# Scatters over four gate tables in turns, and attention scores of two heads at a time

## The chip, the cores and the metric

The kernel runs on one core of one Trainium2 chip. The metric is device time in microseconds (us) of one execution; of the kernel before it is the median of three runs. One execution was also recorded by the hardware profiler, and every duration below is from that recording.

The core's engines work side by side, each through its own instructions in order: TensorE (PE; its weight loads are PEld), VectorE (DVE), ScalarE (ACT), GpSimd (POOL) and SyncE (SP). They wait for each other through semaphores. A DMA is issued by an engine, runs on the DMA engines, and lands later. PE writes into PSUM, from where ACT and DVE fetch results.

## The reference

Two transformer blocks over 256 tokens of width 2048, all in float32. The first block: attention with 16 "forgetting" heads and 16 dilated heads, an output projection, and then PEER, a layer that picks 128 of 16384 experts per token. The second block: sliding-window attention (12 heads), gated linear attention, stick-breaking attention (8 heads), an output projection and a squared-ReLU MLP.

```python
def peer(x, w_query, sub_keys, expert_down, expert_up):     # T = 256 tokens, 8 heads, top 16 of each
    q = (xt @ w_query).reshape(T, PEER_HEADS, 2, PEER_HALF)
    scores = jnp.einsum('thpc,hpnc->thpn', q, sub_keys)
    vals, idx = lax.top_k(scores, PEER_TOPK)
    cand = vals[..., 0, :, None] + vals[..., 1, None, :]    # 16 x 16 sums per head
    top_vals, top_c = lax.top_k(cand, PEER_TOPK)
    experts = i1 * PEER_N_KEYS + i2                         # 8 x 16 experts per token
    gates = jax.nn.softmax(top_vals)
    hdn = jax.nn.gelu(einsum('ted,td->te', expert_down[experts], x))
    return einsum('te,ted->td', gates * hdn, expert_up[experts])

def stick_breaking(q, k, v):                                # per head
    z = q @ k.T * scale
    between = reversed_cumsum(log_sigmoid(-z)) - log_sigmoid(-z)
    return where(strict, exp(log_sigmoid(z) + between), 0) @ v
```

## The kernel before

**The matrix products.** All large products run as one stream of steps on PE (class Gemm, function run). A step is half of a weight tile of 1 MB: SP loads the tile (raw), ACT rounds it to a high part (whi), DVE computes the low part (wlo <- raw, whi), and PE does 12 matmuls with 512 columns, or in the products called turned 8 with 512 and 8 with 256, into acc. Up to four steps are split ahead. The stages in order: projections of block one (96 steps), its output projection (32), the PEER query (32), the products with all of expert_down (256 steps in 16 chunks, called s1 below) and with all of expert_up (256 steps, s2), the projections of block two (80), its output projection (32) and the MLP (256).

**The rest rides along.** Everything else is written as generators in lanes (evac, main, tail, attn, choose, top, rows). After every PE step one round goes through the lanes; a generator emits some instructions and says with `yield n` how many rounds later it wants to go on. This settles at build time the order in which each engine gets its instructions. A virtual clock per engine (vt), advanced by a fixed price per instruction, decides a few things, such as whether a low part is given to POOL. Nearly all instructions carry line 195, that of the helper which records them; those that issue DMAs on POOL carry their own lines.

**PEER.** The kernel computes the products with all 16384 experts and multiplies by a table of gates that is zero for the experts not picked. For each of four query groups g and two token halves tt, a generator `choose` finds the 16 best of each head on DVE. Its 32 columns of experts and gates are then scattered by 32 indirect DMAs on POOL (line 1096), each of which adds one gate per token into a DRAM table. There are four tables, gates00, gates01, gates10 and gates11, chosen by g mod 2 and tt. Two scatters into one table must not overlap, so the second waits on POOL until the first has landed; scatters into different tables don't wait for each other. Before, each of the eight sets of 32 was a generator of its own in the lane rows (up to four active), which emitted one scatter per round. There are 256 scatters.

When s1 is nearly done, `weigh` fetches for each chunk c the activations (line 1124) and the rows of the four tables (line 1127) on POOL's queue, adds two halves on POOL (nb <- nb,nb), multiplies on DVE (nb <- nb,nb), and splits the result into xt, which s2 reads. The call for chunk 0 stands behind all scatters in POOL's order; its multiplication, and behind one more low part that of chunk 1, stand in DVE's order some 20 steps before the end of the 256 steps of s1, among the low parts of the weights.

**Attention.** Dilated, sliding-window and stick-breaking heads are worked in pairs: the 128 partitions of a tile qk hold two heads of 64 rows each. `dil_pair`, `swa_pair` and `stick_pair` transpose (aux <- const,nb), copy to qk, and then did one head per round: two score matmuls (aux <- qk, 64 rows deep, 128 and 256 columns), then the softmax on DVE and ACT, and a `tail` that transposes the probabilities and multiplies by v. In stick_head the scores z go through three ACT operations, two of DVE and a mask on POOL (nb <- nb,const) to l1m; two rounds later PE multiplies l1m by a triangle (aux <- nb,const, here called the suffix sums).

Of the kernel before, what the change touches and what calls it, by code (L numbers as in the profile page):

```python
# [10 lines left out]
I32 = mybir.dt.int32  # L11
U32 = mybir.dt.uint32
AF = mybir.ActivationFunctionType
OP = mybir.AluOpType
# [4 lines left out]
T = 256  # L19
# [5 lines left out]
CAND = [(0, 1, 16), (1, 1, 8), (2, 1, 5), (3, 1, 4), (4, 1, 3), (5, 3, 2), (8, 8, 1)]  # L25
NCAND = 50
CLAMP = 2.0
MATCH, PACE = 0.09, 2.0
SWA_ORDER = [0, 3, 1, 4, 2, 5, 6, 9, 7, 10, 8, 11]


# [177 lines left out]
class Build:  # L209
# [276 lines left out]
    def attend(self, p, v, out):  # L486

        nc = self.nc
        pt = self.aux([128, 384])
        for i in range(3):  # L490
            nc.tensor.transpose(pt[:, i * 128:(i + 1) * 128], p[:, i * 128:(i + 1) * 128], self.c("ident"))
        ps = p[:, :384]
        nc.vector.tensor_copy(ps, pt)
        yield 1
        po = self.aux([128, 2, 64])
        nc.tensor.matmul(po[:, 0, :], ps[:, :128], v(0), start=True, stop=True)
        nc.tensor.matmul(po[:, 1, :], ps[:, 128:256], v(0), start=True, stop=False)
        nc.tensor.matmul(po[:, 1, :], ps[:, 256:384], v(1), start=False, stop=True)
        nc.vector.tensor_tensor(out, po, p[:, 388:390, None].to_broadcast([128, 2, 64]), op=OP.mult)
        self.pss.give(p)  # L500

    def scores(self, qk, rows):
        nc = self.nc
        sc = self.aux([128, 384])
        nc.tensor.matmul(sc[:, :128], qk[rows, 0, :], qk[rows, 2, :], start=True, stop=True)
        nc.tensor.matmul(sc[:, 128:], qk[rows, 1, :], qk[rows, 2:4, :].rearrange("p a b -> p (a b)"),
                         start=True, stop=True)
        return sc

    def fox_head(self, h, st, cnt):  # L510
        nc = self.nc
        q, k, v = st["fq"], st["fk"], st["fv"]
        while "gate" not in st:
            yield 1
        qk = yield from self.get(self.qks, [128, 4, 128])
        pt = self.aux([128, 4, 128])
        for i, src in enumerate((q, k)):
            for tt in range(2):
                nc.tensor.transpose(pt[:66, 2 * i + tt, :], src[:, tt, h, :], self.c("ident"))
        nc.scalar.activation(qk[:66], pt[:66], AF.Copy)  # L520
        yield 1
        p = yield from self.get(self.pss, [128, 392])
        self.softmax_head(self.scores(qk, slice(0, 66)), self.c("fmask"), p)
        self.qks.give(qk)
        yield 2
        yield from self.attend(p, lambda t: v[:, t, h, :], q[:, :, h, :64])
        cnt[0] += 1

    def dil_pair(self, i, q, k, v, cnt):
        nc = self.nc  # L530
        qk = yield from self.get(self.qks, [128, 4, 128])
        pt = self.aux([128, 4, 128])
        for j, src in enumerate((q, k)):
            for tt in range(2):
                nc.tensor.transpose(pt[:, 2 * j + tt, :],
                                    src[:, tt, 2 * i:2 * i + 2, :].rearrange("p a b -> p (a b)"), self.c("ident"))
        nc.scalar.activation(qk, pt, AF.Copy)
        yield 1
        for j in range(2):
            p = yield from self.get(self.pss, [128, 392])  # L540
            self.softmax_head(self.scores(qk, slice(64 * j, 64 * j + 64)), self.c("dmask"), p)
            self.add("tail", self.tail(p, v, 2 * i + j, q, cnt))
            yield 1
        self.qks.give(qk)

    def tail(self, p, v, h, out, cnt):
        yield 1
# [26 lines left out]
    def body(self):  # L574
        from contextlib import ExitStack
        with ExitStack() as ctx:
            tc = self.tc
            self.cp = ctx.enter_context(tc.tile_pool(name="cp", bufs=1))
            self.sm = ctx.enter_context(tc.tile_pool(name="sm", bufs=1))
            self.wp = ctx.enter_context(tc.tile_pool(name="wp", bufs=1))  # L580
            self.xp = ctx.enter_context(tc.tile_pool(name="xp", bufs=1))
            self.np = ctx.enter_context(tc.tile_pool(name="np", bufs=1))
            self.wk = ctx.enter_context(tc.tile_pool(name="wk", bufs=1))
            self.hgt, self.hgs = None, deque()
            self.ph = None
            self.ps = ctx.enter_context(tc.tile_pool(name="ps", bufs=1, space=PSUM))
            self.dr = ctx.enter_context(tc.tile_pool(name="dr", bufs=1, space=DRAM))
            ctx.enter_context(tc.manual_schedule())
            self.xs = Slots(self.xp, "xt", 3)
            self.nb = Slots(self.np, "nb", 7)  # L590
            self.lane("evac", 2, 2)
            self.lane("main", 8, 1)
            self.lane("tail", 4, 4)
            self.lane("attn", 2, 1)
            self.lane("choose", 1, 1, True)
            self.lane("top", 2, 2, True)
            self.lane("rows", 4, 2)
            self.program()
            self.phase(None)

# [282 lines left out]
    def peer(self, hn, st):  # L883
# [8 lines left out]
        def begin():  # L892
            assert not any(self.lanes[l]["queue"] or self.lanes[l]["active"] for l in ("attn", "tail"))
            self.phase("query")
            self.share = 1e9
            p = self.pp
            st["keys"] = self.nb.take([128, 2048])
            nc.gpsimd.dma_start(st["keys"], ins["keys"])
            st["top"] = self.nb.take([128, 3, 2, 8, 2, 16])
            st["pick"] = self.nb.take([128, 768])  # L900
            st["pk"] = st["pick"][:, :512].rearrange("p (t i n) -> p t i n", t=2, i=2)
            st["v"], st["ixf"] = st["top"][:, 0], st["top"][:, 1]
            st["ix"] = st["top"][:, 2].bitcast(U32)
            self.eqs = Slots(p, "eq", 2)
            st["oh"] = self.xs.take([128, 4096])
            st["q"], st["qT"], st["sc"] = (deque(st["oh"][:, 512 * i:512 * i + 512] for i in r)
                                           for r in ((0, 1, 2, 3), (4, 5), (6, 7)))
# [115 lines left out]
    def choose(self, g, tt, st, topn, done):  # L1023
# [62 lines left out]
        nc.vector.tensor_scalar(ix, e.rearrange("p a b -> p (a b)"), 128.0, self.c("row"), op0=OP.mult, op1=OP.add)  # L1086
        if g == 3 and tt == 1:
            self.nb.give(st["top"])
        self.add("rows", self.scatter(g, tt, st, done))

    def scatter(self, g, tt, st, done):

        nc = self.nc
        gd = st["gd"][g % 2, tt].rearrange("e (t o) -> (e t) o", o=1)
        for c in range(32 * g, 32 * g + 32):
            nc.gpsimd.indirect_dma_start(  # L1096
                out=gd, out_offset=bass.IndirectOffsetOnAxis(ap=st["pk"][:, tt, 0, c:c + 1].bitcast(I32), axis=0),
                in_=st["pk"][:, tt, 1, c:c + 1], in_offset=None, compute_op=OP.add)
            yield 1
        done["rows"] += 32  # L1100
        if done["rows"] == T:
            self.share = 2.0

    def zero_gates(self, st):

# [470 lines left out]
    def swa_pair(self, i, st, bt, sk, oa, cnt):  # L1576
# [9 lines left out]
        for j in range(2):  # L1586
            h = SWA_ORDER[2 * i + j]
            p = yield from self.get(self.pss, [128, 392])
            self.softmax_head(self.scores(qk, slice(64 * j, 64 * j + 64)), bt[h // 6][:, h % 6, :], p,
                              (sk[:, 0, h:h + 1], sk[:, 1, h:h + 1]))  # L1590
# [44 lines left out]
    def stick_pair(self, i, st, oc, cnt):  # L1635
# [13 lines left out]
    def stick_head(self, qk, rows, s, h, st, oc, cnt, j):  # L1649

        nc = self.nc
        L, lb, l1m = s[:, 0], s[:, 1], s[:, 2]
# [1 line left out]

        def diag(a):
            return a.rearrange("p (a b) -> p a b", a=3)[:, 0:3:2, :]
        z = self.aux([128, 384])
        nc.tensor.matmul(z[:, :256], qk[rows, 2, :], qk[rows, 0:2, :].rearrange("p a b -> p (a b)"),
                         start=True, stop=True)
        nc.tensor.matmul(z[:, 256:], qk[rows, 3, :], qk[rows, 1, :], start=True, stop=True)  # L1660
        if j:
            self.qks.give(qk)
# [3 lines left out]
        yield 2  # L1666
# [44 lines left out]
```

## Time and profile before

| | |
|---|---|
| median of three runs | 3154.98 us (3150.28 to 3162.14) |
| the profiled execution | 3151.58 us, span 3149.8 us |
| PE busy | 3056.1 us, 97% of the span |
| DVE, ACT, POOL busy | 64%, 45%, 24% |
| granted TensorE clock, mean of the span | 0.988 |
| chain that ended last: PE acc | 65% |
| same chain: DMA gates<-nb (scatters landing) | 12% |
| same chain: POOL gates L1096 (scatters issued) | 5% |
| same chain: DMA nb<-gates | 3% |
| scatters (L1096): 256 | 474.5 us busy, 411.4 us of POOL idle before them |

The profile's chain of waits is followed back from the last instruction, so a share in it is time that the end waited for, at one point or another. An engine's idle time is put down to what ended it.

### The profile page before, as it was taken

What the parts mean: (1) busy time and instruction counts of PE and PEld (TensorE: products, weight loads), DVE (VectorE), ACT (ScalarE), POOL (GpSimd) and SP (SyncE); (2) the same over time, 40 slices, a digit from 0 to 9 for tenths busy, and PEclk for the clock granted to TensorE, in tenths of its full rate; (3) what the DMA queues carried; (4) which work ended last, traced back from release to release, by engine and by line L of the source; (5) the groups of instructions that cost most, each with busy time, mean ns of one, the idle gap of its engine ahead of it and who ended that gap; (6) DMA issues with size and microseconds to landing.
All of it is one profiled execution on the core that took longest, in us unless ns stands there. A gap on an engine that the chain in (4) does not pass through costs nothing.

```text
span 3149.8 us, 39414 instructions
## 1 busy us (share of the span) xinstructions
PE 3056.1 (97%) x15388; PEld 2574.3 (82%) x15388; DVE 2008.5 (64%) x2908; ACT 1429.5 (45%) x1918; POOL 744.8 (24%) x503
## 2 busy tenths in 40 slices
PE   8999999999999995699999999999999999999998
PEld 6888888888888884678888888877888888888887
DVE  4555668999555552677676765655757555555565
ACT  4445444555444442334444444554545444444443
POOL 3011201687665764343122110000111000000000
PEclk9999999999999997899999999999999999999999
DMA  9556954677777775788777755454444455555554
GB/s 347 220 174 222 329 179 167 193 201 228 213 213 213 212 215 131 258 298 290 278 255 274 272 201 197 174 204 147 168 168 174 171 191 194 193 187 188 192 194 147
DMA packets 157530, 667.32 MB, mean 212 GB/s; under 512 B 48944, under 2 KB 65756, under 8 KB 90144
## 3 DMA queue, kind: packets, MB, share of 16 engines
q1 hardware_dynamic: 77984, 551.64, 49.1%
q0 software_dynamic: 61808, 96.32, 12.4%
q10 hardware_dynamic: 17552, 16.85, 1.6%
q8 instruction: 121, 1.98, 0.2%
q14 instruction: 65, 0.53, 0.0%
HBM read 612.16 MB, written 54.94 MB: 212 GB/s over the span
## 4 chain that ended last, share of the span: by engine, by line
PE 70%; DMA 16%; POOL 7%; DVE 4%; issue 3%; ACT 1%; DVEq 0%; POOLq 0%; SPq 0%; ACTq 0%
PE acc L195 65%; DMA gates<-nb 12%; POOL gates L1096 5%; PE aux L195 5%; DMA nb<-gates 3%; DVE wlo L195 2%; DVE nb L195 1%; POOL nb L1127 0%; ACT whi L195 0%; POOL nb L195 0%; DVE xt L195 0%; DMA raw<-in_w 0%; DMA raw<-in_wu 0%; DVE tt L195 0%; DVE tmp L195 0%
## 5 line engine op out<-in xcount | busy, mean ns | idle before, releaser
L195 DVE TENSOR_TENSOR wlo<-raw,whi 128x1024 fp32r<-128x1024 f32 x1038 | 1299.8, 1255 | 838.2 <-ACT whi L195 829.2
L195 PE MATMUL acc<-whi,xt 128*128 128x512 f32 x5248 | 1666.7, 394 | 1.9 <-ACT whi L195 1.6
L195 ACT ACTIVATE whi<-raw 128x1024 fp32r<-128x1024 f32 x1040 | 1094.3, 1057 | 944.3 <-PE acc L195 853.6
L195 PEld LDWEIGHTS acc<-whi,xt 128*128 128x128 f32 x5248 | 987.1, 188 | 215.1 <-issue 6.0
L195 PE MATMUL acc<-wlo,xt 128*128 128x512 f32 x2624 | 1024.7, 391 | 5.9 <-POOL wlo L195 4.1
L195 PE MATMUL acc<-xt,whi 128*128 128x512 f32 x3072 | 772.3, 393 | 3.1 <-DVE xt L195 3.1
L195 PEld LDWEIGHTS acc<-xt,whi 128*128 128x128 f32 x3072 | 554.6, 189 | 103.1 <-DVE xt L195 3.3
L195 PEld LDWEIGHTS acc<-wlo,xt 128*128 128x128 f32 x2624 | 494.2, 188 | 108.9 <-DVE wlo L195 5.4
L1096 POOL DMA_INDIRECT gates<-nb x256 | 474.5, 1853 | 411.4 <-DMA gates<-nb 204.7
L195 PEld LDWEIGHTS acc<-xt,wlo 128*128 128x128 f32 x3072 | 420.9, 191 | 91.9 <-DVE wlo L195 62.2
L195 PE MATMUL acc<-xt,wlo 128*128 128x256 f32 x3072 | 431.3, 283 | 60.1 <-DVE wlo L195 60.0
L195 ACT ACTIVATE tmp<-tmp 128x512 f32<-128x512 f32 (+5 forms) x84 | 46.5, 554 | 216.0 <-DVE tmp L195 215.8
L195 POOL TENSOR_TENSOR nb<-nb,nb 128x1024 f32<-128x1024 f32 (+1 forms) x34 | 93.8, 2777 | 201.9 <-DMA nb<-gates 169.9
L195 DVE TENSOR_TENSOR nb<-nb,nb 128x1024 f32<-128x1024 f32 (+2 forms) x42 | 54.6, 1308 | 68.8 <-POOL nb L195 68.8
L1127 POOL DMA_DIRECT2D nb<-gates x64 | 56.8, 920 | 172.3 <-DVE nb L195 131.4
L195 ACT ACTIVATE tmp<-acc 128x256 f32<-128x256 f32 x128 | 41.8, 378 | 105.2 <-PE acc L195 105.2
L195 DVE TENSOR_TENSOR h<-h,acc 128x512 f32<-128x512 f32 x136 | 86.8, 679 | 0.0
L195 ACT ACTIVATE p<-p 128x128 f32<-128x128 f32 x88 | 39.4, 449 | 81.8 <-DVE p L195 81.8
L195 ACT ACTIVATE xt<-aux 128x512 fp32r<-128x512 f32 (+2 forms) x70 | 39.7, 584 | 76.3 <-PE aux L195 76.0
L195 POOL TENSOR_TENSOR tmp<-nb,const 128x64 f32<-128x64 f32 x32 | 11.2, 379 | 231.3 <-ACT nb L195 231.3
L195 DVE TENSOR_TENSOR xt<-nb,xt 128x1024 fp32r<-128x1024 f32 x48 | 62.6, 1307 | 2.5 <-ACT xt L195 2.5
L195 ACT ACTIVATE xt<-nb 128x1024 fp32r<-128x1024 f32 x48 | 50.3, 1053 | 30.2 <-PE acc L195 30.2
(232 smaller groups left out, 1267.6 us busy)
## 6 DMA issues: line engine op xcount, KB each, us to landing
raw<-in_wd SPq DMA_DIRECT2D x128, 1024.0 KB
raw<-in_wu SPq DMA_DIRECT2D x128, 1024.0 KB
raw<-in_wm SPq DMA_DIRECT2D x128, 1024.0 KB
raw<-in_w SPq DMA_DIRECT2D x87, 1024.0 KB
gates<-const POOLq DMA_DIRECT2D x32, 1024.0 KB
raw<-in_wo SPq DMA_DIRECT2D x32, 1024.0 KB
nb<-gates POOLq DMA_DIRECT2D x64, 512.0 KB
raw<-in_wq SPq DMA_DIRECT2D x16, 1024.0 KB
```

The lines of the kernel that those rows point to most:

```text
L195: return f(*a, **k)
L1096: nc.gpsimd.indirect_dma_start(out=gd, out_offset=bass.IndirectOffsetOnAxis(ap=st["pk"][:, tt, 0, c:c + 1].bitcast(I32), axis=0), in_=st[" ...
L1127: nc.gpsimd.dma_start(g[:, :, 128 * tt:128 * tt + 128], st["gd"][hf, tt][CH * c:CH * c + CH].rearrange("(a p) t -> p a t", p=128))
```

## The change

Three edits. **Scatters:** one generator takes the chosen sets from a list (`st["chosen"]`), keeps up to four of them in turns, and emits one scatter of each in rotation, at a price of 1.9 us of POOL's virtual clock per scatter, no longer one per round and set. **Scores:** dilated, sliding-window and stick-breaking pairs take two buffers at once and emit the score matmuls of both heads in one round, those with equal shapes next to each other, before the softmax of either. **Rounds:** `attend` waits two rounds, not one, between the transposed probabilities and the product with v; in stick_head the first part is called directly by the pair, and its rest enters the lane tail.

```diff
-MATCH, PACE = 0.09, 2.0
+MATCH, PACE, SCATTER = 0.09, 2.0, 1.9
...
         nc.vector.tensor_copy(ps, pt)
-        yield 1
+        yield 2
         po = self.aux([128, 2, 64])
...
-    def scores(self, qk, rows):
+    def scores(self, qk, *rows):
         nc = self.nc
-        sc = self.aux([128, 384])
-        nc.tensor.matmul(sc[:, :128], qk[rows, 0, :], qk[rows, 2, :], start=True, stop=True)
-        nc.tensor.matmul(sc[:, 128:], qk[rows, 1, :], qk[rows, 2:4, :].rearrange("p a b -> p (a b)"),
-                         start=True, stop=True)
+        sc = [self.aux([128, 384]) for _ in rows]
+        for x, r in zip(sc, rows):
+            nc.tensor.matmul(x[:, :128], qk[r, 0, :], qk[r, 2, :], start=True, stop=True)
+        for x, r in zip(sc, rows):
+            nc.tensor.matmul(x[:, 128:], qk[r, 1, :], qk[r, 2:4, :].rearrange("p a b -> p (a b)"),
+                             start=True, stop=True)
         return sc
...
-        for j in range(2):
-            p = yield from self.get(self.pss, [128, 392])
-            self.softmax_head(self.scores(qk, slice(64 * j, 64 * j + 64)), self.c("dmask"), p)
+        while len(self.pss.free) < 2:
+            yield 1
+        ps = [self.pss.take([128, 392]) for _ in range(2)]
+        for j, (p, sc) in enumerate(zip(ps, self.scores(qk, slice(0, 64), slice(64, 128)))):
+            self.softmax_head(sc, self.c("dmask"), p)
             self.add("tail", self.tail(p, v, 2 * i + j, q, cnt))
-            yield 1
         self.qks.give(qk)
+        yield 2
...
-            self.lane("rows", 4, 2)
+            self.lane("rows", 1, 1)
...
-        self.add("rows", self.scatter(g, tt, st, done))
+        st["chosen"].append((g, tt))
...
-        for c in range(32 * g, 32 * g + 32):
-            nc.gpsimd.indirect_dma_start(
-                out=gd, out_offset=..., in_=st["pk"][:, tt, 1, c:c + 1], in_offset=None, compute_op=OP.add)
-            yield 1
-        done["rows"] += 32
-        if done["rows"] == T:
-            self.share = 2.0
+    def scatter(self, st, done):
+        nc, vt = self.nc, self.vt
+        turns = deque()
+        while done["rows"] < T:
+            while st["chosen"] and len(turns) < 4:
+                g, tt = st["chosen"].popleft()
+                turns.append((g, tt, st["gd"][g % 2, tt].rearrange("e (t o) -> (e t) o", o=1),
+                              deque(range(32 * g, 32 * g + 32))))
+            vt["POOL"] = max(vt["POOL"], vt["PE"] - CLAMP)
+            while turns and vt["POOL"] - vt["PE"] < SCATTER:
+                g, tt, gd, left = turns.popleft()
+                c = left.popleft()
+                nc.gpsimd.indirect_dma_start(
+                    out=gd, out_offset=..., in_=st["pk"][:, tt, 1, c:c + 1], in_offset=None, compute_op=OP.add)
+                vt["POOL"] += SCATTER
+                done["rows"] += 1
+                if left:
+                    turns.append((g, tt, gd, left))
+            yield 1
+        self.share = 2.0
...
+        while len(self.sbs.free) < 2:
+            yield 1
+        ss = [self.sbs.take([128, 3, 384]) for _ in range(2)]
+        zs = [self.aux([128, 384]) for _ in range(2)]
+        rows = (slice(0, 64), slice(64, 128))
+        for z, r in zip(zs, rows):
+            nc.tensor.matmul(z[:, :256], qk[r, 2, :], ...)
+        for z, r in zip(zs, rows):
+            nc.tensor.matmul(z[:, 256:], qk[r, 3, :], qk[r, 1, :], start=True, stop=True)
+        self.qks.give(qk)
         for j in range(2):
-            s = yield from self.get(self.sbs, [128, 3, 384])
-            self.add("tail", self.stick_head(qk, slice(64 * j, 64 * j + 64), s, 2 * i + j, st, oc, cnt, j))
-            yield 1
+            g = self.stick_head(zs[j], ss[j], 2 * i + j, st, oc, cnt)
+            next(g)
+            self.add("tail", g)
+        yield 2
```

(swa_pair changes as dil_pair does; the `yield 2` behind the first part of stick_head becomes a `yield 3`, whose number the direct `next(g)` does not use.)

The order on POOL, about 110 scatters in, before the change; the names are the four gate tables:

```order
L1096 DMA gates00_188<-nb4_14_3632 2097152x1
L1096 DMA gates11_191<-nb4_14_3632 2097152x1
L1096 DMA gates00_188<-nb4_14_3632 2097152x1
L1096 DMA gates11_191<-nb4_14_3632 2097152x1
L1096 DMA gates00_188<-nb4_14_3632 2097152x1
L1096 DMA gates11_191<-nb4_14_3632 2097152x1
L1096 DMA gates00_188<-nb4_14_3632 2097152x1
L1096 DMA gates11_191<-nb4_14_3632 2097152x1
```

The same place on POOL after the change:

```order
L1112 DMA gates11_191<-nb4_14_3632 2097152x1
L1112 DMA gates00_188<-nb4_14_3632 2097152x1
L1112 DMA gates10_190<-nb4_14_3632 2097152x1
L1112 DMA gates01_189<-nb4_14_3632 2097152x1
L1112 DMA gates11_191<-nb4_14_3632 2097152x1
L1112 DMA gates00_188<-nb4_14_3632 2097152x1
L1112 DMA gates10_190<-nb4_14_3632 2097152x1
L1112 DMA gates01_189<-nb4_14_3632 2097152x1
```

Two tables alternated; now all four do. Counted over the whole order by how far back the last scatter into the same table stands: before 17 scatters directly behind one of the same table, 108 two behind and 123 three behind; after 19, 34, 59 and 139 (four behind).

The order on PE in the second block, at the first stick-breaking heads, before the change (qk_1 and qk_2 are two pairs; nb_79 is l1m of the first head):

```order
L195 MATMUL aux<-qk_2_18372 128x256
L195 MATMUL aux<-qk_2_18372 128x128
L195 MATMUL acc<-whi,xt_28_17488 128x512
L195 MATMUL acc<-wlo,xt_28_17488 128x512
L195 MATMUL acc<-whi,xt_28_17488 128x512 x2
L195 MATMUL acc<-wlo,xt_28_17488 128x512
L195 MATMUL acc<-whi,xt_28_17488 128x512 x2
L195 MATMUL acc<-wlo,xt_28_17488 128x512
L195 MATMUL acc<-whi,xt_28_17488 128x512 x2
L195 MATMUL acc<-wlo,xt_28_17488 128x512
L195 MATMUL acc<-whi,xt_28_17488 128x512
L195 MATMUL aux<-nb_79_18371,const 128x128 x4
```

The head of nb_79 was scored one step earlier than the rows shown here, so two steps of acc lie between its scores and its suffix sums. The same stretch for the second pair after the change (nb_81 is l1m of its first head):

```order
L195 MATMUL aux<-qk_2_18391 128x128 x2
L195 MATMUL aux<-const,nb_71_16260 128x128 x4
L195 MATMUL acc<-whi,xt_28_17488 128x512
L195 MATMUL acc<-wlo,xt_28_17488 128x512
L195 MATMUL acc<-whi,xt_28_17488 128x512 x2
L195 MATMUL acc<-wlo,xt_28_17488 128x512
L195 MATMUL acc<-whi,xt_28_17488 128x512 x2
L195 MATMUL acc<-wlo,xt_28_17488 128x512
L195 MATMUL acc<-whi,xt_28_17488 128x512 x2
L195 MATMUL acc<-wlo,xt_28_17488 128x512
L195 MATMUL acc<-whi,xt_28_17488 128x512
L195 MATMUL aux<-nb_81_18480,const 128x128 x4
```

The scores of both heads stand together, and one step of acc, not two, lies between them and the suffix sums.

## Rows read from the trace of the kernel before

**Rows 1.** Windows of 79 us: PE, PEld, DVE, ACT, POOL busy (count), granted clock, DMA share, GB/s

```profile
1106.00:1185.00 79.00, 79.00 (x453) 69.49 (x452) 44.05 (x52) 37.22 (x49) 50.63 (x27) 1.00 0.75 211
1185.00:1264.00 79.00, 39.60 (x227) 34.49 (x225) 18.85 (x19) 15.95 (x21) 40.15 (x27) 0.77 0.49 129
```

**Rows 2.** Timeline of PE, end of s1: start, us, engine, line, operation, shape, count [idle before <-releaser]

```profile
1222.60 2.00 PE L195 MATMUL acc<-xt,whi 128*128 128x512 f32 x8
1265.69 2.07 PE L195 MATMUL acc<-xt,wlo 128*128 128x256 f32 x8 [41.09 <-DVE wlo L195]
1288.89 2.08 PE L195 MATMUL acc<-xt,wlo 128*128 128x256 f32 x8 [18.74 <-DVE wlo L195]
1349.01 0.79 PE L195 MATMUL acc<-wlo,xt 128*128 128x512 f32 x1 [4.13 <-POOL wlo L195]
```

**Rows 3.** Timeline of DVE, the same stretch

```profile
1211.76 1.24 DVE L195 TENSOR_TENSOR wlo<-raw,whi 128x1024 fp32r<-128x1024 f32 x1 [1.51 <-ACT whi L195]
1261.15 3.35 DVE L195 TENSOR_TENSOR nb<-nb,nb 128x1024 f32<-128x1024 f32 x1 [48.14 <-POOL nb L195]
1282.21 3.35 DVE L195 TENSOR_TENSOR nb<-nb,nb 128x1024 f32<-128x1024 f32 x1 [14.06 <-POOL nb L195]
```

**Rows 4.** Timeline of POOL, the same stretch

```profile
1243.53 1.54 POOL L1096 DMA_INDIRECT gates<-nb  x1 [1.62 <-DMA gates<-nb]
1258.78 4.63 POOL L195 TENSOR_TENSOR nb<-nb,nb 128x1024 f32<-128x1024 f32 x2 [9.18 <-DMA nb<-gates]
1279.85 4.63 POOL L195 TENSOR_TENSOR nb<-nb,nb 128x1024 f32<-128x1024 f32 x2 [12.08 <-DMA nb<-gates]
1312.90 4.76 POOL L195 TENSOR_TENSOR nb<-nb,nb 128x1024 f32<-128x1024 f32 x2 [20.79 <-DMA nb<-gates]
```

**Rows 5.** View of the tile gates: durations in ns, and POOL's idle time (us, times)

```profile
L1096 POOL DMA_INDIRECT gates<-nb x256: 1538/1606/3034, 524.1 to 1243.5; - x128
...
  DMA gates<-nb: 204.7, 118
```

**Rows 6.** Timeline of POOL, scatters at the ends of three stretches

```profile
524.11 1.70 POOL L1096 DMA_INDIRECT gates<-nb  x1 [164.89 <-DVE nb L195]
564.53 1.54 POOL L1096 DMA_INDIRECT gates<-nb  x1 [3.73 <-DMA gates<-nb]
1068.33 1.54 POOL L1096 DMA_INDIRECT gates<-nb  x1 [0.30 <-issue]
1116.77 1.54 POOL L1096 DMA_INDIRECT gates<-nb  x1 [0.30 <-issue]
1211.75 1.54 POOL L1096 DMA_INDIRECT gates<-nb  x1 [1.78 <-DMA gates<-nb]
```

**Rows 7.** Chain of waits in order of time, landings of scatters: start, us, what

```profile
806.86 8.14 DMA gates<-nb
1221.26 2.85 DMA gates<-nb
```

**Rows 8.** Timeline of DVE, the last result of choose

```profile
764.03 0.24 DVE L195 TENSOR_SCALAR nb<-tt,const 128x32 int32<-128x32 f32 x1
```

**Rows 9.** Timeline of PE and POOL, stick-breaking heads (a float32 matmul has two records)

```profile
2330.78 0.92 PE L195 MATMUL aux<-qk 64*128 64x256 f32 x4
2331.62 0.50 PE L195 MATMUL acc<-whi,xt 128*128 128x512 f32 x1
2334.59 0.93 PE L195 MATMUL aux<-qk 64*128 64x256 f32 x8
2335.45 0.50 PE L195 MATMUL acc<-whi,xt 128*128 128x512 f32 x1
2340.04 1.56 POOL L195 TENSOR_TENSOR nb<-nb,const 128x256 f32<-128x256 f32 x1 [0.86 <-DVE nb L195]
2342.44 1.95 PE L195 MATMUL aux<-nb,const 128*128 128x128 f32 x16
```

More of the change, by code (lines that the diff above doesn't have):

```diff
@@ L522, in fox_head @@
         p = yield from self.get(self.pss, [128, 392])
-        self.softmax_head(self.scores(qk, slice(0, 66)), self.c("fmask"), p)
+        self.softmax_head(self.scores(qk, slice(0, 66))[0], self.c("fmask"), p)
         self.qks.give(qk)
@@ L904, in begin @@
             self.eqs = Slots(p, "eq", 2)
+            st["chosen"] = deque()
+            self.add("rows", self.scatter(st, done))
             st["oh"] = self.xs.take([128, 4096])
@@ L1088, in choose @@
             self.nb.give(st["top"])
-        self.add("rows", self.scatter(g, tt, st, done))
-    def scatter(self, g, tt, st, done):
-        nc = self.nc
-        gd = st["gd"][g % 2, tt].rearrange("e (t o) -> (e t) o", o=1)
-        for c in range(32 * g, 32 * g + 32):
-            nc.gpsimd.indirect_dma_start(
-                out=gd, out_offset=bass.IndirectOffsetOnAxis(ap=st["pk"][:, tt, 0, c:c + 1].bitcast(I32), axis=0),
-                in_=st["pk"][:, tt, 1, c:c + 1], in_offset=None, compute_op=OP.add)
+        st["chosen"].append((g, tt))
[12 more added lines that the diff above has]
+                nc.gpsimd.indirect_dma_start(
+                    out=gd, out_offset=bass.IndirectOffsetOnAxis(ap=st["pk"][:, tt, 0, c:c + 1].bitcast(I32), axis=0),
+                    in_=st["pk"][:, tt, 1, c:c + 1], in_offset=None, compute_op=OP.add)
+                vt["POOL"] += SCATTER
+                done["rows"] += 1
+                if left:
+                    turns.append((g, tt, gd, left))
             yield 1
-        done["rows"] += 32
-        if done["rows"] == T:
-            self.share = 2.0
+        self.share = 2.0
     def zero_gates(self, st):
@@ L1585, in swa_pair @@
         yield 1
-        for j in range(2):
+        while len(self.pss.free) < 2:
+            yield 1
+        ps = [self.pss.take([128, 392]) for _ in range(2)]
+        for j, (p, sc) in enumerate(zip(ps, self.scores(qk, slice(0, 64), slice(64, 128)))):
             h = SWA_ORDER[2 * i + j]
-            p = yield from self.get(self.pss, [128, 392])
-            self.softmax_head(self.scores(qk, slice(64 * j, 64 * j + 64)), bt[h // 6][:, h % 6, :], p,
-                              (sk[:, 0, h:h + 1], sk[:, 1, h:h + 1]))
+            self.softmax_head(sc, bt[h // 6][:, h % 6, :], p, (sk[:, 0, h:h + 1], sk[:, 1, h:h + 1]))
             kv = h // 3
@@ L1643, in stick_pair, with stick_head @@
         yield 1
-        for j in range(2):
-            s = yield from self.get(self.sbs, [128, 3, 384])
-            self.add("tail", self.stick_head(qk, slice(64 * j, 64 * j + 64), s, 2 * i + j, st, oc, cnt, j))
-            yield 1
-    def stick_head(self, qk, rows, s, h, st, oc, cnt, j):
+        while len(self.sbs.free) < 2:
[4 more added lines that the diff above has]
+        for z, r in zip(zs, rows):
+            nc.tensor.matmul(z[:, :256], qk[r, 2, :], qk[r, 0:2, :].rearrange("p a b -> p (a b)"),
+                             start=True, stop=True)
+        for z, r in zip(zs, rows):
+            nc.tensor.matmul(z[:, 256:], qk[r, 3, :], qk[r, 1, :], start=True, stop=True)
+        self.qks.give(qk)
+        for j in range(2):
+            g = self.stick_head(zs[j], ss[j], 2 * i + j, st, oc, cnt)
+            next(g)
+            self.add("tail", g)
+        yield 2
+    def stick_head(self, z, s, h, st, oc, cnt):
         nc = self.nc
@@ L1656, in diag @@
             return a.rearrange("p (a b) -> p a b", a=3)[:, 0:3:2, :]
[L1657 to L1662, printed above, removed]
         self.log_sigmoid(lb, z, L)
@@ L1665, in stick_head @@
         nc.gpsimd.tensor_tensor(diag(l1m), diag(l1m), mask, op=OP.mult)
-        yield 2
+        yield 3
         bt = self.aux([128, 384])
```

## The prediction

> **What bounds the kernel now.** I read the page first: PE is busy for 3056.1 of 3149.8 us, so at most some 94 us of PE's idle time and what a lowered clock costs can be won without taking work from PE. The windows then show where: until 1185 us PE is busy without a gap at clock 1.00, and in the next window it works 39.6 of 79 us at 0.77 [rows 1]. The timeline of PE gives three waits there, 41.09, 18.74 and 4.13 us, the first two on a low part from DVE [rows 2]. DVE was not slow: it stood from 1213.0 to 1261.15 at the multiplication of chunk 0 and then 14.06 us at that of chunk 1, both times for POOL [rows 3]. POOL in turn issued its last scatter at 1243.53, and only then could it fetch and add chunk 0 (add at 1258.78) and chunk 1 (1279.85) [rows 4]. So the end of s1 waits for the 256 scatters, which begin at 524.11 and end at 1243.53. choose is done at 764.03 [rows 8], long before: after that only POOL's own pace counts. That pace has two parts: the issue (median 1.606 us) and 204.7 us of POOL's waiting, 118 times, for an earlier scatter into the same table to land [rows 5].
>
> **Scatters.** The step from scatter to scatter can be read by how many tables take turns [rows 6]. One table: eight steps from 524.11 to 564.53, 5.05 us each. Two: 30 steps from 1116.77 to 1211.75, 3.17 us. Three: 21 steps from 1068.33 to 1116.77, 2.31 us. Four tables don't occur before. From below the step is the shortest issue plus the 0.30 us that POOL takes between two, 1.54 + 0.30 = 1.84 us [rows 5, 6]. From above the trace gives no end, since landing might slow with more in flight; if it does not, three tables' 2.31 us is the end. Landing took 2.85 us when nothing else moved and 8.14 us among weight loads [rows 7]; four steps of 2.3 us are 9.2 us, so most scatters would find their table free. I take 2.30 us, next to the row of three tables, because there already the issue and not the landing sets most steps.
>
> The Trainium skill, page "DMA: Bandwidth & Descriptors", section "SWDGE vs HWDGE vs iDMA", says that only one queue is allocated to the DMAs whose descriptors GpSimd writes. By that rule all scatters share one line, and a fourth table adds waiting in line but no pace: the step would be that of three tables, or worse. The rows bear it out so far only in that landings among other traffic are long; what it would give is the third rival below.
>
> The order after the change has 13 steps of one table, 18 of two, 60 of three, 141 of four (mixed-in first scatters counted with their neighbours), then 17 of two and 6 of one. The sum: 13 x 5.05 = 66, 18 x 3.17 = 57, 60 x 2.40 = 144, 141 x 2.30 = 324, 17 x 3.17 = 54, 6 x 5.05 = 30, together 675 us; for three tables I take 2.40, since the steps during choose are longer. The same prices give before 8 x 5.05 + 108 x 3.17 + 130 x 2.40 + 9 x 3.5 = 726 us against 719.4 recorded, 7 too many. So the last scatter comes 51 us earlier by the sums, 48 us if I take something off for the mismatch: at about 1195 us.
>
> What this is worth at PE: chunk 0 and chunk 1 move with it, but their fetches now run beside weight loads, which PE's standing still had kept away. POOL waited 9.18 and 12.08 us for the first two fetches, and 20.79 us for the third, when weights flowed again [rows 4]. From 0 to 9 us more for each; I take 5 and 3, since PE still stops during the second. Chunk 0 is then added 43 us earlier, at about 1220 instead of 1263, which DVE still waits for but PE, with work until 1224.6 [rows 2], hardly does. The second wait keeps its size: PE went on at 1288.89 after chunk 1, and now does 48 - 8 = 40 us earlier, at about 1249. The 4.13 us wait is a fetch of a later chunk and stays. The lowered clock around the standstills (0.77 over that window [rows 1]) shortens with them; I count nothing for it, since one standstill is left. Gain: 40 us.
>
> From the other sides: with 1.84 us a step the last scatter is 65 us earlier still (141 x 0.46), both waits vanish, and the gain is 41.1 + 18.7 and the slow matmuls, about 62 us, perhaps 66 with the third wait. With a step of 2.60 us it is 42 us later, and nothing is left.
>
> **Scores of two heads.** PE took 0.84 us from the start of one head's scores to the next product (2330.78 to 2331.62), and 0.86 us where two heads of different halves of the partitions happened to stand together (2334.59 to 2335.45) [rows 9]: the second head is free. In the trace there are 28 such groups for 36 heads, 20 of one head (x4) and 8 of two (x8). After the change each of 18 pairs is one group. Ten groups go, at 0.85 us and about 0.1 us for the change to the smaller tile and back: 9.5 us less on PE, which is the bound there. Alternating by shape within the group should change nothing; were the overlap lost by it, it would cost 18 x 0.85 = 15 us.
>
> **Rounds.** In attend the extra round lengthens a head's way by one step of about 3 us. The heads' ends stand before the same steps of PE as before (dilated, sliding-window) or four steps later (forgetting heads, with more than 20 steps to spare), and PE hardly waits in attention now; 0 us, from -2 to +2.
>
> In stick_head it goes the other way: only one step now lies between scores and suffix sums. For the group of two heads at 2334.59 the second head's l1m was ready when POOL's mask ended, 2340.04 + 1.56 = 2341.60, so 7.0 us after its scores began [rows 9]; before, PE came to the suffix sums at 2342.44 and had no wait. Now PE gets there after 0.86 us of scores, some 0.45 us of transposes, one step of 2.97 us (2331.62 to 2334.59) and 0.5 us of the first head's sums: 4.8 us. It waits 2.2 us, and all of PE's queue with it; four pairs make about 9 us. Bounds: 0 (ACT takes the six operations sooner) to 4 x 4 = 16.
>
> **Sum.** 3151.6 for the profiled execution - 40 - 9.5 + 9 = 3111; it stood 3.4 us below the median of its runs, so against the median 3114 us.
>
> **The rivals.**
> 1. Forecast, 3095 to 3132, chance 0.57.
> 2. Four tables let POOL issue at its shortest, near 1.9 us, and both waits at the end of s1 vanish: -62 and 0 from attention, 3155 - 62 = 3093, with the third wait and no wait in stick_head down to 3080. For it: the median issue is 1.606 us [rows 5], so 1.91 us a step. Against: in the stretch of three tables steps average 2.31. Chance 0.18.
> 3. One line for all scatters: the fourth table gives little. At 2.40 a step the last scatter is 14 us later than forecast, 3128; at 2.60 the gain is gone, 3155. For it: landing is long when much is in flight [rows 7]. Against: two tables to three brought 3.17 to 2.31. Chance 0.17 for 3132 to 3160, of which half is within 0.5% of before.
> 4. Slower: landing stretches with each table in flight. The step of four tables then is a quarter of the landing, and from 10.5 us on (2.6 x 4) the scatters end later than before; at 12 us the step is 3.0, the last scatter 141 x 0.7 = 99 us later than forecast, and the time 3114 + 99 = 3213, less what PE gains by fetches without traffic. For it: 2.85 us alone against 8.14. Against: with three tables in flight the landing must have stayed near 7 us to allow 2.31 x 3. Chance 0.05.
> 5. The edit doesn't bring four tables into turns: the order shows that it does; 0.03, with a time as before.
>
> The attention edits alone move each of these by -8 to +12 us.
>
> **From these the numbers.** The range that leaves out no more than 2 in 10 reaches from the second case's 3085 to the third's 3144. A difference below 0.5%, 16 us, I can't tell from none in this kernel. Faster by more (below 3139): cases 1, 2 and half of 3, 0.57 + 0.18 + 0.10 = 0.85; within 0.5%: 0.09; slower by more: 0.06.
>
> **What would show it.** In the profile after: scatters in the middle about 2.3 us apart, hardly any of them waiting for a landing; the last one near 1195 us; PE's first wait at the end of s1 gone or below 5 us, the second near 20 us, ending near 1249; 18 groups of scores, each eight records in about 0.86 us; four waits of PE at suffix sums in the stick-breaking heads, about 2 us each, released by POOL. I am wrong if scatters with four tables in turns still wait for landings, if the second wait vanishes, or if PE waits anywhere in the first block's attention.

## The result, and the profile after

The changed kernel takes 3108.83 us (median of 4 runs, 3107.26 to 3116.25); the kernel before, run beside it on the same chip, takes 3155.95 us. The ratio is 0.9855, 95% interval 0.983 to 0.9879. The forecast was 3114 us in a range of 3085 to 3144, faster. The execution profiled after has a span of 3106.7 us, 43.1 less than before.

The same two windows as in [rows 1], with the same columns:

```profile
1106.00:1185.00 79.00, 79.00 (x455) 69.57 (x454) 43.52 (x51) 37.95 (x50) 35.71 (x21) 1.00 0.74 215
1185.00:1264.00 79.00, 63.99 (x352) 55.85 (x351) 47.08 (x42) 29.44 (x39) 28.44 (x21) 0.89 0.82 282
```

PE works 63.99 us of the second window instead of 39.60, at a mean granted clock of 0.89 instead of 0.77. Its timeline there, to be read beside [rows 2], has two waits instead of three:

```profile
1240.69 2.08 PE L195 MATMUL acc<-xt,wlo 128*128 128x256 f32 x8 [15.01 <-DVE wlo L195]
1301.41 0.79 PE L195 MATMUL acc<-wlo,xt 128*128 128x512 f32 x1 [3.98 <-POOL wlo L195]
```

The 41.09 us wait is gone, 15.01 remain of 18.74, and the third is as it was. Behind it stands POOL, to be read beside [rows 4]: the last scatter and the additions of chunks 0, 1 and 2.

```profile
1187.72 1.54 POOL L1112 DMA_INDIRECT gates<-nb  x1 [3.73 <-PE acc L195]
...
1209.59 5.75 POOL L195 TENSOR_TENSOR nb<-nb,nb 128x1024 f32<-128x1024 f32 x2 [14.58 <-DMA nb<-gates]
...
1231.65 4.63 POOL L195 TENSOR_TENSOR nb<-nb,nb 128x1024 f32<-128x1024 f32 x2 [11.98 <-DMA nb<-gates]
1236.24 3.32 POOL L195 TENSOR_TENSOR wlo<-raw,whi 128x1024 fp32r<-128x1024 f32 x1
...
1265.17 4.75 POOL L195 TENSOR_TENSOR nb<-nb,nb 128x1024 f32<-128x1024 f32 x2 [21.25 <-DMA nb<-gates]
```

Between the two stands DVE, to be read beside [rows 3]. It no longer waits at the product of chunk 0; it stands 13.94 us at that of chunk 1, and the low part behind that product ends at 1240.64, when PE goes on:

```profile
1218.86 1.22 DVE L195 TENSOR_TENSOR nb<-nb,nb 128x1024 f32<-128x1024 f32 x1
1234.02 3.35 DVE L195 TENSOR_TENSOR nb<-nb,nb 128x1024 f32<-128x1024 f32 x1 [13.94 <-POOL nb L195]
1237.28 3.36 DVE L195 TENSOR_TENSOR wlo<-raw,whi 128x1024 fp32r<-128x1024 f32 x1
```

The last two also run 3.35 and 3.36 us, beside POOL's additions and POOL's own low part, where the product at 1218.86 took 1.22 us. So some 4 of the 15 us that PE waits are not waiting for a fetch at all.

The last scatter is 55.8 us earlier. The view of the tile gates [rows 5] shows both sides of it: 56 waits for a landing instead of 118, and a longer median issue, 1.830 us instead of 1.606.

```profile
L1112 POOL DMA_INDIRECT gates<-nb x256: 1538/1830/3037, 522.4 to 1187.7; - x128
...
  DMA gates<-nb: 117.6, 56
```

Where the 43.1 us came from is read by the start of the same work in both traces. PE rows of before (the first product of s2; the first transposes of the sliding-window heads, of the stick-breaking heads, and of what follows these):

```profile
1333.59 0.40 PE L195 MATMUL acc<-whi,xt 128*128 128x512 f32 x1
2228.84 0.60 PE L195 MATMUL aux<-const,nb 128*128 128x128 f32 x4
2323.69 0.66 PE L195 MATMUL aux<-const,nb 128*128 128x128 f32 x4 [0.80 <-DVE xt L195]
2437.48 1.03 PE L195 MATMUL aux<-const,nb 128*128 128x128 f32 x8
```

The same four places after:

```profile
1286.13 0.40 PE L195 MATMUL acc<-whi,xt 128*128 128x512 f32 x1
2181.99 0.60 PE L195 MATMUL aux<-const,nb 128*128 128x128 f32 x4
2276.24 0.66 PE L195 MATMUL aux<-const,nb 128*128 128x128 f32 x4 [0.80 <-DVE xt L195]
2393.02 1.04 PE L195 MATMUL aux<-const,nb 128*128 128x128 f32 x8
```

| stage | change, us | worked out |
|---|---|---|
| first block, to the first scatter | -1.7 | 522.40 against 524.11 |
| scatters and rest of s1 | -45.7 | 1286.13 - 522.40 against 1333.59 - 524.11 |
| s2 | +0.6 | 895.86 against 895.25 |
| sliding-window heads | -0.6 | 94.25 against 94.85 |
| stick-breaking heads | +3.0 | 116.78 against 113.79 |
| the rest | +1.4 | 713.68 against 712.32 |

The whole gain lies in the scatters' stage; the attention edits come to nothing.

### The profile page after: what moved, and what is told of

Its sections match the earlier page's. It is cut to its first block, busy times and chain, and to the rows that moved or that the text cites. A ratio compares the mean times of both kernels' runs of the same rounds, so it can differ in the third digit from the quotient of the medians.

```text
span 3106.7 us, 39401 instructions
## 1 busy us (share of the span) xinstructions
PE 3050.9 (98%) x15388; PEld 2570.5 (83%) x15388; DVE 2010.1 (65%) x2908; ACT 1430.7 (46%) x1918; POOL 757.4 (24%) x503
## 5 line engine op out<-in xcount | busy, mean ns | idle before, releaser
L1112 POOL DMA_INDIRECT gates<-nb x256 | 486.1, 1899 | 343.5 <-DVE nb L195 162.7
```

Source lines behind the costliest of these rows:

```text
L1112: nc.gpsimd.indirect_dma_start(out=gd, out_offset=bass.IndirectOffsetOnAxis(ap=st["pk"][:, tt, 0, c:c + 1].bitcast(I32), axis=0), in_=st[" ...
```

## The experiments

Theory: the number of tables in turns sets the step from scatter to scatter, the last scatter sets PE's waits at the end of s1, and the attention edits cancel. Rivals: attention carries part of the gain; turns alone suffice, however many tables; the remaining wait belongs to something other than the scatters. Times are medians, ratios are to runs of the kernel before on the same chip.

**One part of the change at a time.** The kernel before with the new scatter only:

```diff
...
-        self.add("rows", self.scatter(g, tt, st, done))
+        st["chosen"].append((g, tt))
...
```

> The kernel before with the new scatters alone (four sets in turns), attention as before. Theory: the whole gain comes from the end of the scatters, and the attention edits together are worth about nothing. Then the last scatter comes near 1189 us, PE waits once (about 15 us) for DVE's product of chunk 1, and the time is 46 to 48 us below before: about 3109, ratio 0.985. By the terms of the forecast (scatters -40, scores -9.5, stick-breaking +9) it would be 3115. Rival: the attention edits carry a good part of the gain; then this kernel stays above 3120.

3112.96 us, ratio 0.987 (0.9843 to 0.9897): the gain is in the scatters. In its profile the last scatter is at 1194.80, the two waits are 1.62 and 19.89 us. And the kernel after with the old scatter, the same lines reversed:

> The kernel after with the scatters of before: the attention edits alone. Theory: the shared score groups save 4 to 7 us of PE, new waits (PE for ACT's and DVE's work before the scores, PE for POOL's mask before the suffix sums) take as much back; 3152 to 3158, ratio 0.999 to 1.001, with PE's three waits at the end of s1 as before (41, 19 and 4 us). By the terms of the forecast: -9.5 + 9 = -0.5, so 3155. Rival (they carry part of the gain): 3145 or less.

3152.88 us, ratio 1.0003 (0.9987 to 1.0019): no difference, as the theory and the forecast's terms had it. The rival that attention helps falls.

**How many tables.** A price of 0.7 us for a scatter on the virtual clock by which the kernel's planner settles the order:

```diff
-MATCH, PACE, SCATTER = 0.09, 2.0, 1.9
+MATCH, PACE, SCATTER = 0.09, 2.0, 0.7
```

> The kernel after with 0.7 us in place of 1.9 us as the planner's cost of one scatter, so that sets are worked off sooner after they are chosen and fewer of them meet in turns. Theory (the gain comes from the number of tables in turns, and the cost 1.9 is what makes four meet): the steps are again those of one to three tables (5.0, 3.1, 2.4 us), the last scatter comes 20 to 50 us later than in the kernel after (1210 to 1240), and the time is 3130 to 3155. Rival (turns between whatever sets there are suffice, the cost matters little): last scatter by 1200, 3110 to 3120. A third: scatters issued sooner get ahead of everything and POOL is done earlier than 1187, below 3105.

3544.11 us, ratio 1.1242 (1.1218 to 1.1266). All three expectations missed, far off: I had counted on one to three tables in turns. At that pace the planner places all 32 scatters of a set before the next set is chosen, and the sets go one table after the other to the end. It is the plainest sign that the tables matter: only the order of the 256 scatters differs, and everything else on POOL, DVE and ACT keeps its order. The view of the tile gates of this kernel has 248 waits for a landing (second row), and below it the timeline of PE has a standstill of 430 us:

```profile
L1112 POOL DMA_INDIRECT gates<-nb x256: 1538/1538/2610, 521.9 to 1630.7; - x128
...
  DMA gates<-nb: 684.8, 248
```

```profile
1652.57 2.07 PE L195 MATMUL acc<-xt,wlo 128*128 128x256 f32 x8 [430.20 <-DVE wlo L195]
```

Three sets at most:

```diff
-            while st["chosen"] and len(turns) < 4:
+            while st["chosen"] and len(turns) < 3:
```

> The kernel after with three sets in turns at most instead of four; about 200 of the 256 scatters then go through three tables. Theory (from three tables on the issue on POOL sets the step): 2.3 to 2.45 us a step instead of 2.24 in that stretch, some 10 to 25 us later at the last scatter, 1200 to 1215; the time goes with it, 3115 to 3135. Rival (the fourth table is what removes the wait for landing): steps of 2.7 us or more, last scatter near 1240, 3150. A third (rotation alone, the number above two does not matter): as after, 3105 to 3112.

3141.55 us, ratio 0.9969 (0.9956 to 0.9982). The steps are near what the theory had (2.26 to 2.50 us by stretch with three tables, 2.36 over all), but the last scatter came at 1225.31, 10 us past its range, and the time 6 us past it: I had left out the tail. There 19 steps of two tables (3.36 us) and 13 of one (5.03) take 129.2 us, where the same 32 scatters take 108.2 us in the kernel after. So of the 37.6 us between the two last scatters 21 lie in the tail and 16.6 before it, and of these 5 in the first 13 steps, which are alike in both kernels (5.47 us a step against 5.02): some 11 us are left for the shorter step.

The next scatter to the table with most still to come, among those not used in the last two:

```diff
-        turns = deque()
+        turns, recent = deque(), []
...
-                g, tt, gd, left = turns.popleft()
+                fresh = [x for x in turns if (x[0] % 2, x[1]) not in recent[-2:]] or [turns[0]]
+                x = max(fresh, key=lambda x: 64 - recent.count((x[0] % 2, x[1])))
+                turns.remove(x)
+                g, tt, gd, left = x
+                recent.append((g % 2, tt))
```

> The kernel after, but the next scatter goes to the table with the most scatters still to come, among those not used in the last two, so that four tables last until the end. Theory (the number of tables in turns sets the step: 4.3 to 5 us with one, 3.1 with two, 2.2 to 2.4 with three or four): the tail of the kernel after, 31 steps of 2.46, 17 of 3.10 and 6 of 5.64 us, becomes 54 steps of 2.24, which takes 42 us out; some of it is lost in the middle, where three tables take turns longer. Last scatter 1150 to 1165, PE's wait of 15 us at the end of s1 gone, 3088 to 3097 in all, ratio about 0.98. Rival (chunk 1 is late by its own fetch and add on POOL, not by the scatters): the wait keeps 10 us or more, 3103 to 3112.

3092.91 us, ratio 0.9811 (0.9783 to 0.9839), last scatter at 1163.38. The last 67 steps take 2.23 us each, and the 15 us wait is 2.31; the third wait, for POOL, grew from 3.98 to 7.62. The theory holds, and the price of the tail is shown.

Put together, last scatter (view of gates) against the span:

| kernel | last scatter | span |
|---|---|---|
| one table (pace 0.7) | 1630.7 | 3542.1 |
| before | 1243.5 | 3149.8 |
| three tables | 1225.3 | 3139.3 |
| scatters alone | 1194.8 | 3109.3 |
| after | 1187.7 | 3106.7 |
| most left first | 1163.4 | 3092.9 |

From before to one table 387.2 us later cost 392.3; from before to after 55.8 us earlier gave 43.1; from after to most left first another 24.3 us earlier gave 13.8, since PE then waits little. Each span is that of one execution, and executions of the kernel before lie 12 us and more apart, so small differences in the table say nothing.

**Whose wait the 15 us are.** DVE's products later in its order, scatters unchanged:

```diff
-        yield 9
+        yield 15
         for i in (0, 4):
             nc.vector.tensor_tensor(al[:, i:i + 4], al[:, i:i + 4], g0[:, i:i + 4], op=OP.mult)
```

> The kernel after, with DVE's products of chunks 0 to 3 six steps of PE's program later in its order; the scatters are as in the kernel after. Theory (PE's 15 us wait is not for the gates, but for weights that DVE splits behind a product at which it stands): last scatter 1188 to 1200 as before, the wait below 3 us, 3088 to 3100. Rival (the results of the chunk are needed by then, or POOL's next chunk is held up by the later product): the wait only moves, 3105 to 3120.

3107.75 us, ratio 0.9863 (0.9837 to 0.9889): no gain, the rival's number; the theory's, 3088 to 3100 with a wait below 3 us, missed. The profile shows both at work. The wait fell to 5.77 us and s2 began 10.1 us earlier (1276.04 instead of 1286.13); then a wait of 11.62 us at 1389.60 gave it back. The two rows in its timeline of PE:

```profile
1248.09 2.08 PE L195 MATMUL acc<-xt,wlo 128*128 128x256 f32 x8 [5.77 <-DVE wlo L195]
...
1389.60 0.80 PE L195 MATMUL acc<-wlo,xt 128*128 128x512 f32 x1 [11.62 <-POOL wlo L195]
```

The timeline of POOL in the same kernel says why: a low part of a weight, which the planner had put on POOL, stood behind the addition of a chunk that waited 17.69 us for its fetch.

```profile
1382.62 4.63 POOL L195 TENSOR_TENSOR nb<-nb,nb 128x1024 f32<-128x1024 f32 x2 [17.69 <-DMA nb<-gates]
1387.21 2.33 POOL L195 TENSOR_TENSOR wlo<-raw,whi 128x1024 fp32r<-128x1024 f32 x1
```

So the same with the two low parts on DVE (the planner may use POOL for them again only from the last chunk on):

```diff
-        self.share = 2.0
...
-        yield 9
+        if CH * (c + 1) == NE:
+            self.share = 2.0
+        yield 15
```

> The kernel with the products six steps later, and with the two low parts of weights that the planner had put on POOL between the chunks' additions (3.3 us each) on DVE instead. Theory: the later product did take 10 us out of PE's wait at the end of s1 (s2 began at 1276.0 instead of 1286.1), and an 11.6 us wait at 1389.6 gave them back, because a low part that PE needs stood on POOL behind an addition that waited for a fetch; without it the 10 us stay: 3092 to 3099. Rival (PE is held in s2 by the chunks' own pace on POOL, about 28 us each, whatever else stands there): 3103 to 3110, with waits of PE for DVE's product or split of a later chunk in its place.

3094.19 us, ratio 0.9827 (0.9801 to 0.9854): the theory's number. PE has no wait for POOL's low part left, and 7.32 us for DVE's. This kernel and the last two below ran on a chip on which the kernel before took 3149.11 us, so against the kernel after the ratios are to be compared, 0.9827 with 0.9855; PE's waits around the start of s2 (1200 to 1400 us) are 9.1 us together instead of 19.3. A good part of the wait in the kernel after was thus DVE standing in its order, not the gates being needed by PE; it could be moved, but only paid once the next one behind POOL was gone. The two low parts on DVE without the later products were not run; the rows of the kernel after give that at most the 3.98 us wait for POOL and the 2.1 us by which DVE's low part is longer beside POOL's.

**The suffix sums** one step of PE later:

```diff
-            self.add("tail", g)
+            self.add("tail", self.later(g))
...
+    def later(self, g):
+        yield 1
+        yield from g
```

> The kernel after, with the suffix sums and what follows of each stick-breaking head one step of PE's program later. Theory: the waits of PE for POOL's mask (eight, together 4.4 us in the kernel after) go, and nothing else moves: 3 to 4 us less than after in the stretch of the stick-breaking heads, 3105 in all, ratio 0.9845. By the forecast (9 us of waits) it would be 9 us less, 3100. Rival: the heads' ends move past the point where the next product needs them, and a wait comes there instead: not less than after.

3107.48 us, ratio 0.9849 (0.9826 to 0.9872): by the time alone nothing is told, since in its profile the last scatter fell at 1199.85 with the same order of scatters. The stage tells it. From this kernel's timeline of PE, the start of the stick-breaking heads, the suffix sums of their first pair, and the start of what follows:

```profile
2287.59 0.66 PE L195 MATMUL aux<-const,nb 128*128 128x128 f32 x4 [0.80 <-DVE xt L195]
...
2298.36 1.95 PE L195 MATMUL aux<-nb,const 128*128 128x128 f32 x16
...
2398.20 1.03 PE L195 MATMUL aux<-const,nb 128*128 128x128 f32 x8
```

110.61 us against 116.78 after and 113.79 before, and no wait for POOL's mask. Leaving out the step between scores and sums thus cost 6.2 us, more than the 3 to 4 that I expected of this run and less than the forecast's 9. Of it 4.4 us show as waits; most of the rest is that a pair's sums now come in two groups of 1.16 us (rows in the next section), where they are one group of 1.95 us here.

**Together.** Most left first with the later sums (the two diffs above):

> Both the suffix sums one step later and the table with the most left first. Theory: the two gains lie in different stretches and add up: 6 us in the stick-breaking heads, the wait of 15 us at the end of s1 gone; 3082 to 3091, ratio 0.977 to 0.980. Rival (the time won at the end of s1 is given back later, at the fetches of the next chunks): 3095 to 3105.

3084.63 us, ratio 0.979 (0.9762 to 0.9817). The gains add up. With the low parts on DVE as well:

> The suffix sums later, the table with the most left first, and the two low parts on DVE instead of POOL. Theory: PE's wait for POOL's low part (4.9 us in the kernel without this edit) goes: 3078 to 3083. Rival (DVE has no room for them there): as without the edit, 3083 to 3088, or more.

3077.75 us, ratio 0.9777 (0.975 to 0.9805), at the lower edge of the theory's 3078 to 3083. And with the later products too:

> As the run before, and the products six steps later as well. Theory: with the scatters done by 1160 hardly a wait is left for the later product to take away: within 3 us of the run before, 3076 to 3084. Rival (a chunk's result comes too late for s2 when its product is later): 3085 or more.

3076.34 us (3076.15 to 3076.67), ratio 0.9771 (0.9745 to 0.9796): the fastest, though not told apart from the one before it. PE is busy 99% of the span, and its costliest wait is one at the very start that the kernel before had as well (8.1 us, for DVE's xt). The first line of its page:

```profile
PE 3041.2 (99%) x15388; PEld 2565.5 (83%) x15388; DVE 2009.1 (65%) x2910; ACT 1429.8 (47%) x1918; POOL 757.8 (25%) x501
```

## Why the prediction was right, step by step

**The last scatter.** Forecast near 1195, measured 1187.72; four other profiles with the same order of scatters have it at 1187.65 to 1199.85, so the forecast lies within their spread. The four-table step was taken as 2.30 us and is 2.24: 127 steps, from these two rows of POOL's timeline after (the scatter before the first of them starts at 740.39):

```profile
742.24 1.54 POOL L1112 DMA_INDIRECT gates<-nb  x1 [0.30 <-issue]
...
1024.90 2.02 POOL L1112 DMA_INDIRECT gates<-nb  x1 [0.30 <-issue]
```

Four of the 127 wait for a landing, so the issue sets the step, as the forecast chose. Other prices held too: one table 5.02 us at the start and 5.64 in the last six steps (forecast 5.05), two 2.89 to 3.10 (3.17), three 2.20 to 2.46 (2.40). The time of rival 3, one line for all scatters, did not come, since steps of 2.40 us or more did not. That the step hardly shrinks was true of it: 2.24 us against 2.26 to 2.50 in the kernel with three tables. What the fourth table removes is the waiting: 4 of 127 steps wait for a landing, where 10 of the 31 steps of three tables that follow them do. The Trainium skill, page "DMA: Bandwidth & Descriptors", section "SWDGE vs HWDGE vs iDMA", has one queue for these DMAs, the rule from which the rival came; these steps don't decide whether there is one, since the issue already sets their pace. Rival 2, the shortest issue of 1.54 us throughout, failed because the issue's mean in that stretch is 1.93 us.

**The gain at PE.** Forecast 40, measured 45.7 in that stage. Two terms were mis-sized: the last scatter, 7 us earlier than forecast, and the second fetch. I charged 5 us more for the first fetch and 3 for the second. The waits before the additions are 14.58 and 11.98 us, against 9.18 and 12.08 [rows 4], so 5.4 and nothing. PE resumed at 1240.69, not 1249: 7 us from the earlier scatter and 3 from the second fetch, less an addition of chunk 0 that took 5.75 us instead of 4.63. The waits before s2 fell by 44.8 us (41.09 + 18.74 - 15.01); only 0.9 us are left for the slower matmuls around them, for which I had counted nothing.

**Scores.** Forecast -9.5, and 16 of the 18 groups do take 0.86 us for two heads, as in the timeline of PE after from one row's start to the next's:

```profile
2322.34 0.92 PE L195 MATMUL aux<-qk 64*128 64x256 f32 x8
2323.20 0.50 PE L195 MATMUL acc<-whi,xt 128*128 128x512 f32 x1
```

One takes 1.05 us, and one 1.94, torn in two by a wait of 0.60 us for DVE's xt. The groups' sum went from 23.9 us (28 groups) to 16.7, so -7.2. The stages show less, because PE now meets waits that it did not have, such as these two, for ACT's copy of q and k and for the softmax of the second head, which began with the first:

```profile
265.16 0.93 PE L195 MATMUL aux<-qk 64*128 64x128 f32 x8 [0.24 <-ACT qk L195]
...
2217.57 0.66 PE L195 MATMUL aux<-const,nb 128*128 128x128 f32 x4 [0.99 <-DVE p L195]
```

**Suffix sums.** Forecast four waits, together 9 us; there are eight, together 4.4 us, here those of the last pair:

```profile
2327.15 1.16 PE L195 MATMUL aux<-nb,const 128*128 128x128 f32 x8 [0.94 <-POOL nb L195]
2329.47 1.16 PE L195 MATMUL aux<-nb,const 128*128 128x128 f32 x8 [1.16 <-POOL nb L195]
```

The place, the releaser and the sign were right, the size half. The term that was too large is the second head's way through ACT, DVE and POOL, taken as 7.0 us from the start of the scores: PE could go on after 6.1 to 6.3 us in three pairs and 7.1 in the last. By the stage the edit costs 6.2 us. So the attention terms were -9.5 + 9 where about -7 + 6 and some new waits are found: two terms that were both too large, with a right sum by luck.

**What I had as wrong-if.** PE does wait in the first block's attention now (0.24 us in the row above), which I had said would prove me wrong; it is too small to matter, and the bound should have had a size. The chances were also added up loosely: half of rival 3 is 0.085, and with rival 5, a time as before, about 0.115 lay within 0.5%, not 0.09.

## What to carry to other kernels

Where a chain of small dependent transfers paces an engine, count the targets in turns for each stretch, the last one above all: an order that keeps them all busy to the end was worth another 14 us here (spans of 3106.7 and 3092.9). A planner's cost decides such an order as much as its rule does: a cost too small by a factor of 2.7 brought the targets one after the other and 435 us. A wait that is moved pays only if the next one in line is off the path, so read on in the trace to where the gain is given back.

## What the runs showed of the hardware

A scatter lands much sooner when the other work stops. With one table the step is 5.27 to 5.71 us while PE works and weights stream (124 steps), and 3.27 to 3.30 us while PE stands (124 steps from 1220.76 on). The windows of that kernel show the two conditions; the last columns are the granted clock, the DMA share and GB/s:

```profile
1050.00:1210.00 160.00, 160.00 (x918) 140.78 (x917) 88.10 (x100) 75.80 (x100) 54.66 (x29) 1.00 0.70 214
1210.00:1640.00 430.00, 12.37 (x70) 10.47 (x68) 0.79 (x1) 2.66 (x4) 204.07 (x135) 0.52 0.15 6
```

PE's work is not what delays it. In the kernel before, a landing took 2.85 us [rows 7] in this stretch, where PE was busy without a gap at clock 1.00 and only the weights, DVE and ACT had stopped:

```profile
1221.00:1224.20 3.20, 3.20 (x19) 2.81 (x18) 0.00 (x0) 0.00 (x0) 1.54 (x1) 1.00 0.12 0
```

That leaves the weights' traffic as the likely cause, which no run separates from DVE's and ACT's work; what DVE does to the issue (1.77 us on average in the first 128 scatters of that one-table kernel, 1.54 in the others) is too little for 2 us.

GpSimd's issue goes with DVE's work. While DVE did nothing in the one-table kernel, all 108 issues took 1.54 us (mean 1539 ns), and PE, which stood too, had the granted clock at 0.50, the lower of its two levels (1.2 GHz):

```profile
1250.00:1600.00 350.00, 0.00 (x0) 0.00 (x0) 0.00 (x0) 0.00 (x0) 166.16 (x108) 0.50 0.14 0
```

In the kernel after, with four tables in turns, they take 1.54 to 2.59 us in a pattern that repeats with DVE's subtractions for the low parts. Its timeline of POOL:

```profile
799.58 1.54 POOL L1112 DMA_INDIRECT gates<-nb  x1 [0.30 <-issue]
801.43 2.03 POOL L1112 DMA_INDIRECT gates<-nb  x1 [0.30 <-issue]
803.76 2.22 POOL L1112 DMA_INDIRECT gates<-nb  x1 [0.30 <-issue]
806.28 1.54 POOL L1112 DMA_INDIRECT gates<-nb  x1 [0.30 <-issue]
808.13 2.32 POOL L1112 DMA_INDIRECT gates<-nb  x1 [0.30 <-issue]
```

Its timeline of DVE beside it:

```profile
800.82 1.23 DVE L195 TENSOR_TENSOR wlo<-raw,whi 128x1024 fp32r<-128x1024 f32 x1 [2.95 <-issue]
...
803.35 1.22 DVE L195 TENSOR_TENSOR wlo<-raw,whi 128x1024 fp32r<-128x1024 f32 x1
...
807.81 1.23 DVE L195 TENSOR_TENSOR wlo<-raw,whi 128x1024 fp32r<-128x1024 f32 x1 [1.51 <-ACT whi L195]
```

The scatters at 801.43, 803.76 and 808.13 start while a subtraction has 0.62, 0.81 and 0.91 us to run, and are 0.49, 0.68 and 0.78 us longer than 1.54: each is held for what is left of it, less 0.13 us. The one at 806.28 starts as another subtraction ends (805.08 to 806.31, not shown here), and is not longer; nor is the one at 799.58, behind whose start a subtraction begins. Of the 175 scatters in that trace that start within a subtraction, 170 fit this within 0.03 us. The Trainium skill, page "DMA: Bandwidth & Descriptors", section "SWDGE vs HWDGE vs iDMA", says that GpSimd writes descriptors into SBUF state which DVE locks it out of during one mode of DVE, its 2-port perf mode. These rows show that GpSimd is held; whether the subtractions ran in that mode they don't show, and no run here varied DVE's work alone.
